# The second branch's merge gates as block products: eight projection slabs per half move into the row phase, and h transposed is written to DRAM

## The chip, the cores and the metric

The kernel runs on one core of one Trainium2 chip. TensorE (PE) multiplies, its weight loads are shown apart (PEld), VectorE (DVE) and ScalarE (ACT) do the elementwise work, GpSimd (POOL) helps both and issues its own DMAs, and SyncE (SP) issues most DMAs. Each engine takes its instructions in the order in which they stand in its queue. The metric is the device time of one launch in microseconds. Before the change the median of three runs is 2776.74 us (2776.49 to 2776.75). What a measurement of this kernel can tell from no change is about 0.2%.

## The reference

One layer of a streaming encoder, in float32, on 2048 prompt frames and 64 sample frames of width 1024:

```
h = rmsnorm(x, norm_g)
[q | k | v | g_a | u | g_b | m] = h @ w_in              # m: two gates of 1024 columns
att = stick_breaking(q, k, v)                           # 8 heads x 128
pb  = multi_scale_pool(u, state) @ w_pool * pool_scale  # windows 2, 4, 8, 16
y_a = (att * silu(g_a)) @ w_br_a
y_b = (pb  * silu(g_b)) @ w_br_b
gate = sigmoid(m)
x = x + (gate[:, :1024] * y_a + gate[:, 1024:] * y_b) @ w_out
y = rmsnorm(x, final_g)
```

The merge gates are the two halves of `sigmoid(m)`: columns 0 to 1023 gate the first branch, columns 1024 to 2047 the second. The sample frames attend to 4096 cached positions as well. Keys, values and the last 15 pooling inputs are outputs too.

## The kernel before, in words

**Numbers.** Every float32 product is made of three fp32r products: each operand is split by `split` (L81, L82) into a rounded part `hi` (ACT) and a rest `lo` (DVE or POOL), and PE adds hi*hi, lo*hi and hi*lo. A matmul here has a 128x128 stationary operand and up to 512 moving columns.

**Halves.** The 2112 rows of activations are worked on in two halves: half A has 1088 rows (1024 prompt rows and the 64 sample rows, in groups of 512, 256 and 320 columns), half B 1024 (two groups of 512). For each half h is built transposed in SBUF (`hhi`, `hlo`): x is loaded and normalised, four PE transposes turn a 128x512 block into the PSUM tile `tr` (two buffers), `split` takes it out (`transposed_h`, L207 on). `build_h0` does so for half A at the very start, `build_h1` for half B in the middle of the kernel.

**Projections.** `proj` (L278) makes 128 output columns of `h @ w_in` for a half, called a slab here: its weights are loaded (`raw`) and split (`whi`, `wlo`), then come 24 matmuls for every group of columns, into the PSUM tile `pj` (two buffers), and an evacuation. For the merge gates `gate_evac` takes a sigmoid on ACT into an `out` tile (L302; three buffers, shared by all that leaves through `outgoing`) and stores it to the DRAM tensor `sm_d`. There are sixteen such slabs per half, eight for each branch.

**What sets the order.** PE's order is written by hand, by generators that `run` interleaves in proportion to their nominal PE time. The order of the other engines is made by a scheduler in the front part of the program, and by hand in the back part. The front part is, in order: the build of h for half A with the first head's projections; attention of half A head by head, with the next head's projections between; the sample attention (`sample_stream`, 36 units of scores, transposes and products, nominal 104.2 us), interleaved with 28 slabs (six branch gates, four pooling groups of two slabs, fourteen merge gates); two more merge gates, interleaved with `build_h1`; attention of half B; branch gates and the pooling groups of half B; and fifteen merge gates (one stands before them), beside which `before_closing` prepares the first weights and rows of the back part.

**A sample unit.** PE makes scores of two heads (`z`, L737 and L738), ACT and DVE fold them into `be` (L742, L743), ACT takes two sigmoids (L569, L570), POOL copies the carry (L574, L581), DVE scans (L579) and multiplies (L582), PE transposes (L770), ACT and DVE split (`a`), and PE multiplies with the split values (L787). A pooling group adds on DVE, for each piece of its two slabs, log2(window) shifted sums (L333) with a few small ones beside them, a combination (L342), a split (`plo`), and later, after PE's mapping products (L388 to L390), a scaling (L392).

**The back part** begins with the row phase: for each branch and each of three strips of 704 rows, seven products of 512x512 blocks (an algorithm that replaces eight block products by seven with sums before and after). `order` lists (branch, strip, product); a step is one such product, 4 x 12 matmuls of 352 columns (`product`, L986 on). Rows come from DRAM (`aT_d`, `bT_d`) as blocks `r11` to `r22`, DVE makes their sums, `make` splits them two steps ahead. `emit` adds, multiplies with the gate loaded from `sm_d` (`sg`), for the second branch adds the first's result (`mp_d`), and stores by a DMA of POOL's queue. Weight blocks and four differences of them (`tw_d`, made by `weight_sums` on POOL or `sums_step` on DVE) are loaded and split by `forms`; `weights_at` says at which half step. After it come the output projection by the same seven products, and the last norm.

## Time and profile before

| what | value |
|---|---|
| median of three runs | 2776.74 us |
| the profiled execution | 2775.71 us, its span 2774.0 us |
| PE busy | 2706.2 us, 98% of the span |
| PEld busy | 2364.5 us |
| DVE busy | 1835.5 us, 66% |
| ACT busy | 1268.3 us, 46% |
| POOL busy | 582.6 us, 21% |
| HBM read, written | 232.46 MB, 108.65 MB |

Stages, by the times of their PE instructions in us from the start of the span: build of h for half A until about 57, attention of half A to 606, sample attention with its slabs to 1067, two merge gates and the build for half B to 1130, attention of half B to 1920, pooling of half B and the first merge gate to 2100, merge gates to 2259, row phase from 2259.87 to 2584.4, output after it.

In a row of the stage view the pairs are busy time and number of instructions of an engine in that stretch, followed by the granted PE clock (1.00 is full speed), the busy share of the DMA engines and what they moved. In a row of a group: source line, engine, operation, output<-inputs, shape and count, then busy time, mean duration in ns and idle time before, with what ended it. In a row of the timeline: start, duration, engine, line, operation, and in brackets the engine's idle time before it and what ended that.

### The profile page before, as it was taken

The numbers are of one execution on the slowest core, as the hardware profiler recorded it, in microseconds if no ns is written. First come the engines' busy times: TensorE is split into PE (matmuls) and PEld (weight loads), VectorE is DVE, ScalarE is ACT, GpSimd is POOL, SyncE is SP. The second block draws the span as 40 slices with busy tenths as digits, with TensorE's granted clock in tenths as the row PEclk, the third lists the DMA queues.
The fourth block names the chain that finished last, engine by engine and source line by source line (L and its number), as shares of the span: only waits on it lengthen the run. The fifth ranks groups of instructions, "written<-read, shape, count | busy, mean of one in ns | idle before, by whom it ended". The sixth has DMA issues, their size and how long they took to land.

```text
span 2774.0 us, 41821 instructions
## 1 busy us (share of the span) xinstructions
PE 2706.2 (98%) x15052; PEld 2364.5 (85%) x15052; DVE 1835.5 (66%) x2843; ACT 1268.3 (46%) x2520; POOL 582.6 (21%) x1285
## 2 busy tenths in 40 slices
PE   6999999999999999999999999999999999999898
PEld 6988888988998989888888888887778889999786
DVE  6555555567777684487878888886453237786776
ACT  4445444455555553355555555554222223333343
POOL 2112222220000001222432343331005501100001
PEclk9999999999999999999999999999999999999999
DMA  5224222234444544311111211112337848776653
GB/s 146 79 81 132 73 72 72 77 98 152 153 156 142 157 141 152 94 46 54 54 46 50 58 54 42 51 39 83 112 99 230 265 161 274 266 258 236 225 159 118
DMA packets 344397, 343.87 MB, mean 124 GB/s; under 512 B 30062, under 2 KB 286558, under 8 KB 344188
## 3 DMA queue, kind: packets, MB, share of 16 engines
q1 hardware_dynamic: 329756, 294.26, 34.2%
q0 software_dynamic: 14432, 46.93, 4.8%
q8 instruction: 118, 1.93, 0.3%
q14 instruction: 91, 0.75, 0.1%
HBM read 232.46 MB, written 108.65 MB: 123 GB/s over the span
## 4 chain that ended last, share of the span: by engine, by line
PE 84%; issue 6%; DVE 5%; DMA 2%; ACT 1%; POOL 1%; SPq 0%; POOLq 0%; DVEq 0%; ACTq 0%
PE pj L284 17%; PE pj L285 17%; PE pj L286 17%; PE tr L638 4%; PE att L655 2%; PE att L654 2%; PE z L627 2%; PE att L653 2%; PE z L626 2%; PE z L625 2%; PE x L989 2%; PE x L991 2%; PE x L993 2%; PE y L989 1%; PE y L993 1%
## 5 line engine op out<-in xcount | busy, mean ns | idle before, releaser
L284 PE MATMUL pj<-hhi,whi 128*128 128x512 f32 (+2 forms) x2608 | 946.5, 363 | 0.0
L286 PE MATMUL pj<-hhi,wlo 128*128 128x512 f32 (+2 forms) x2608 | 918.9, 352 | 0.5 <-DVE wlo L82 0.5
L285 PE MATMUL pj<-hlo,whi 128*128 128x512 f32 (+2 forms) x2608 | 917.7, 352 | 0.1
L286 PEld LDWEIGHTS pj<-hhi,wlo 128*128 128x128 f32 x2608 | 492.7, 189 | 66.1 <-DVE wlo L82 1.0
L284 PEld LDWEIGHTS pj<-hhi,whi 128*128 128x128 f32 x2608 | 495.5, 190 | 59.4 <-ACT hhi L81 0.2
L285 PEld LDWEIGHTS pj<-hlo,whi 128*128 128x128 f32 x2608 | 494.4, 190 | 59.3 <-DVE hlo L82 0.4
L579 DVE TENSOR_TENSOR_SCAN om<-om 128x513 f32<-128x513 f32 (+3 forms) x356 | 387.4, 1088 | 212.1 <-POOL om L561 108.3
L569 ACT ACTIVATE om<-z 128x512 f32<-128x512 f32 (+2 forms) x320 | 171.6, 536 | 322.3 <-PE z L627 272.7
L82 DVE TENSOR_TENSOR wlo<-raw,whi 128x512 fp32r<-128x512 f32 x248 | 179.7, 729 | 194.5 <-ACT whi L81 193.8
L581 POOL COPY carry<-om 128x1 f32<-128x1 f32 x356 | 78.6, 221 | 918.3 <-DVE om L579 870.7
L582 DVE TENSOR_TENSOR be<-be,om 128x512 f32<-128x512 f32 (+3 forms) x356 | 230.2, 647 | 31.5
L81 ACT CAST whi<-raw 128x512 fp32r<-128x512 f32 x256 | 158.2, 623 | 182.2 <-PE pj L285 164.3
L81 ACT CAST a<-tr 128x512 fp32r<-128x512 f32 (+2 forms) x356 | 188.0, 528 | 100.2 <-PE tr L638 89.6
L82 DVE TENSOR_TENSOR a<-tr,a 128x512 fp32r<-128x512 f32 (+2 forms) x356 | 215.2, 605 | 23.8 <-ACT a L81 21.6
L638 PE MATMUL tr<-ident,be 128*128 128x128 f32 x1088 | 175.6, 274 | 6.1 <-DVE be L582 3.6
L638 PEld LDWEIGHTS tr<-ident,be 128*128 128x128 f32 x1088 | 136.1, 140 | 44.7 <-DVE be L582 8.3
L570 ACT ACTIVATE be<-z 128x512 f32<-128x512 f32 (+2 forms) x320 | 170.0, 531 | 0.0
L653 PE MATMUL att<-a,v 128*128 128x512 f32 (+1 forms) x320 | 133.2, 416 | 0.0
L561 POOL TENSOR_SCALAR_AFFINE_SELECT om<-om 128x128 f32<-128x128 f32 x128 | 50.6, 395 | 354.0 <-ACT om L569 353.9
L574 POOL COPY om<-carry 128x1 f32<-128x1 f32 x224 | 124.0, 554 | 2.7 <-DVE be L582 0.7
L655 PE MATMUL att<-a,v 128*128 128x512 f32 (+1 forms) x320 | 118.4, 370 | 3.9 <-DVE a L82 3.6
L654 PE MATMUL att<-a,v 128*128 128x512 f32 (+1 forms) x320 | 117.3, 367 | 0.0
(312 smaller groups left out, 4681.1 us busy)
## 6 DMA issues: line engine op xcount, KB each, us to landing
raw<-in_w_in_dram SPq DMA_DIRECT2D x256, 256.0 KB, 3.2
sg<-sm_d SPq DMA_DIRECT2D x48, 352.0 KB, 5.7
kraw<-in_cache_k_dram SPq DMA_DIRECT2D x64, 256.0 KB, 3.6
vraw<-in_cache_v_dram SPq DMA_DIRECT2D x64, 256.0 KB, 2.9
sm_d<-sgm SPq DMA_DIRECT2D x48, 256.0 KB, 2.4
wraw<-tw_d SPq DMA_DIRECT2D x24, 512.0 KB, 4.1
out_dram<-nat SPq DMA_DIRECT2D x42, 256.0 KB, 2.3
r<-aT_d SPq DMA_DIRECT2D x12, 704.0 KB, 7.1
```

Source lines behind the costliest of these rows:

```text
L81: nc.scalar.copy(hi, src)
L82: (nc.gpsimd if eng == "g" else nc.vector).tensor_tensor(lo, src, hi.bitcast(F32), op=ALU.subtract)
L284: nc.tensor.matmul(ps[:, 0:n], whi[:, k], hhi[:, k, c0:c0 + n], start=k == 0, stop=False)
L285: nc.tensor.matmul(ps[:, 0:n], whi[:, k], hlo[:, k, c0:c0 + n], start=False, stop=False)
L286: nc.tensor.matmul(ps[:, 0:n], wlo[:, k], hhi[:, k, c0:c0 + n], start=False, stop=k == KT - 1)
L569: nc.scalar.activation(om[:, off:512], z[:, off:512], AF.Sigmoid, scale=-SCALE)
L579: nc.vector.tensor_tensor_scan(rev, rev, rev, 1.0, op0=ALU.mult, op1=ALU.bypass)
L582: nc.vector.tensor_tensor(be[:, off:512], be[:, off:512], om[:, off + 1:513], op=ALU.mult)
L638: nc.tensor.transpose(tr[:, i * P:(i + 1) * P], be[:, off + j * P:off + (j + 1) * P], ident)
L653: nc.tensor.matmul(self.acc[:, s], vhi[:, js], ahi[:, s], start=first, stop=False)
L654: nc.tensor.matmul(self.acc[:, s], vlo[:, js], ahi[:, s], start=False, stop=False)
L655: nc.tensor.matmul(self.acc[:, s], vhi[:, js], alo[:, s], start=False, stop=last)
```

## The change

The second branch's eight merge-gate slabs are taken out of both halves' projections. Its gates are computed in the back part instead, by the seven block products, as a new first pass of the row phase (21 steps, before the 42 of the two branches). For this the transposed h must be readable as rows from DRAM, so `transposed_h` gains an ACT copy of `tr` into an `out` tile (`ht`) and a store to the new tensor `hT_d`. The pass takes `hT_d` for its rows, the last 1024 columns of `w_in` for its weights; its `emit` takes a sigmoid on ACT instead of a product on DVE, and writes `sm_d` by POOL's queue. `weight_sums` of the new weights runs on POOL, listed beside the branch gates and pooling groups of half B. Those of the two branch weights, before on POOL beside the merge gates, move to DVE in the new pass (`own_at`, `own`: tiles of the tags `mp` and `mq`).

The list of slabs beside the sample attention is shortened from 28 to 20, with a weight of 22 in `run`; the last pooling group now ends that list.

```diff
-        def transposed_h(i, b, m, xt):
+        def transposed_h(half, i, b, m, xt):
...
             split(hhi[:, b * 4:b * 4 + 4, i * P:i * P + m], hlo[:, b * 4:b * 4 + 4, i * P:i * P + m],
                   trv[:, :, 0:m])
+            ht = outgoing("ht").rearrange("p (j r) -> p j r", j=4)
+            nc.scalar.copy(ht[:, :, 0:m], trv[:, :, 0:m])
+            c0 = half * RA + i * P
+            nc.sync.dma_start(hT_d[b * 512:(b + 1) * 512, c0:c0 + m].rearrange("(j p) r -> p j r", p=P), ht[:, :, 0:m])
...
-            rest.append(proj(GROUPS_A, [merge_gate(0, 3 * g)]))
+            rest += [proj(GROUPS_A, [merge_gate(0, c)]) for c in (2 * g,) if g < 3]
             rest.append(pool_group(0, g))
-            rest += [proj(GROUPS_A, [merge_gate(0, 3 * g + i)]) for i in (1, 2)]
-        rest += [proj(GROUPS_A, [merge_gate(0, c)]) for c in range(12, 2 * KT - 2)]
-        run((sample_stream(), SAMPLE_NS), (chain(*rest), 28.0 * pns))
-        fin = proj(GROUPS_A, [merge_gate(0, c) for c in (2 * KT - 2, 2 * KT - 1)])
+            rest += [proj(GROUPS_A, [merge_gate(0, c)]) for c in (2 * g + 1,) if g < 3]
+        run((sample_stream(), SAMPLE_NS), (chain(*rest), 22.0 * pns))
+        fin = proj(GROUPS_A, [merge_gate(0, c) for c in (KT - 2, KT - 1)])
...
-        run((chain(*rest), 1.0))
+        run((chain(*rest), 13.0), (weight_sums(0), 4.0))
...
-            yield from weight_sums(0)
-            yield from weight_sums(1)
...
-        run((chain(*[proj(GROUPS_B, [merge_gate(1, c)]) for c in range(1, 2 * KT)]), 15 * slab_ns(1)),
-            (before_closing(), 21.0))
+        run((chain(*[proj(GROUPS_B, [merge_gate(1, c)]) for c in range(1, KT)]), 7 * slab_ns(1)),
+            (before_closing(), 13.0))
...
-        order = [(i, t, p) for i in range(2) for t in range(3) for p in range(7)]
+        order = [(i, t, p) for i in range(3) for t in range(3) for p in range(7)]
...
-            src = (aT_d, bT_d)[i]
+            src = (hT_d, aT_d, bT_d)[i]
...
-            nc.vector.tensor_tensor(sg, src, sg, op=ALU.mult)
-            if i:
+            if i == 0:
+                sg = gates.tile([P, 2, NR], F32, name="sg", bufs=5)
+                nc.scalar.activation(sg, src, AF.Sigmoid)
+            else:
+                sg = sgs_.pop(n)
+                nc.vector.tensor_tensor(sg, src, sg, op=ALU.mult)
+            if i == 2:
                 nc.vector.tensor_tensor(sg, sg, mps.pop(n), op=ALU.add)
-            nc.gpsimd.dma_start((mp_d, m_d)[i][c * P:(c + 2) * P, rs].rearrange("(j p) r -> p j r", p=P), sg)
+            dst = (sm_d[D:2 * D], mp_d, m_d)[i]
+            nc.gpsimd.dma_start(dst[c * P:(c + 2) * P, rs].rearrange("(j p) r -> p j r", p=P), sg)
...
+        own_at = {4 * k + 4 * (i - 1) * 4: (i, k) for i in (1, 2) for k in range(4)}
```

**How instructions move, ACT in the first build of h.** The rows are ACT's after the squares of the first two row blocks; `hhi` is the cast out of `tr`, `jk` are sums of squares for later blocks, `sq` is the root that the next normalisation waits for. Before:

```order
L81 CAST hhi<-tr 128x4x128
L177 ACTIVATE jk,acc<-xt 128x512
L81 CAST hhi<-tr 128x4x128
L177 ACTIVATE jk,ss<-xt 128x512
L81 CAST hhi<-tr 128x4x128
L177 ACTIVATE jk,acc<-xt 128x512
L177 ACTIVATE jk,ss<-xt_260 128x512
L88 ACTIVATE sq_96<-sq_95 128x2
```

Now, with what each row waits for (line numbers in rows of the change are the changed file's, up to eight higher here):

```order
L82 CAST hhi<-tr 128x4x128 [waits PE_49]
L216 COPY ht<-tr 128x512 [waits DVE_49]
L178 ACTIVATE jk,acc<-xt 128x512 [waits DMAHW3_49]
L216 COPY ht<-tr 128x512 [waits DVE_49]
L82 CAST hhi<-tr 128x4x128 [waits PE_49]
L178 ACTIVATE jk,ss<-xt 128x512 [waits DMAHW4_49,Activation_49]
L82 CAST hhi<-tr 128x4x128 [waits PE_49]
L216 COPY ht<-tr 128x512 [waits DVE_49]
L178 ACTIVATE jk,acc<-xt 128x512 [waits DMAHW5_49,Activation_49]
L216 COPY ht<-tr 128x512 [waits DMAHW0_49,DVE_49]
L89 ACTIVATE sq_97<-sq_96 128x2 [waits DVE_49]
```

Four copies now stand ahead of the root, and each waits for DVE, which reads the same `tr` for `hlo` first.

**PE at the end of the sample attention.** `z` are a unit's scores, `tr<-ident,be` its transposes, `att` its products, `pj` are slabs. Before, the last unit's scores, transposes and products stand between slab matmuls:

```order
L770 MATMUL tr<-ident,be 128x128 x4
L284 MATMUL pj<-hhi,whi 128x512
L285 MATMUL pj<-hlo,whi 128x512
L286 MATMUL pj<-hhi,wlo 128x512
L284 MATMUL pj<-hhi,whi 128x512
L285 MATMUL pj<-hlo,whi 128x512
L286 MATMUL pj<-hhi,wlo 128x512
L787 MATMUL att<-v_12433,a_12563 128x256 x4
L787 MATMUL att<-v_12438,a_12563 128x256 x4
L284 MATMUL pj<-hhi,whi 128x256
```

Now the last unit runs with nothing between:

```order
L742 MATMUL z<-khi,q_10686 128x512
L743 MATMUL z<-klo,q2h 128x512
L407 MATMUL tr<-ident,shist 15x128
L775 MATMUL tr<-ident,be 128x128 x4
L792 MATMUL att<-v_11677,a_11944 128x256 x4
L792 MATMUL att<-v_11682,a_11944 128x256 x4
L775 MATMUL tr<-ident,be 128x128 x4
L792 MATMUL att<-v_11918,a_12036 128x256 x4
L792 MATMUL att<-v_11923,a_12036 128x256 x4
L792 MATMUL att<-v_12017,a_12052 128x256 x4
L792 MATMUL att<-v_12022,a_12052 128x256 x4
L289 MATMUL pj<-hhi,whi 128x512
```

The slabs ran out with the last pooling group, just ahead of these rows; only the two last merge gates follow.

**POOL in the last head of half B.** `om<-carry` and `carry<-om` are the copies that the scans wait for, `ws` and `tw_d` belong to `weight_sums(0)`. The rows are those of the last five units; before, this place held the copies alone:

```order
L895 DMA ws<-in_w_in_dram 128x512
L579 COPY om<-carry 128x1 x2
L586 COPY carry<-om 128x1
L897 TENSOR_TENSOR ws<-ws 128x512
L586 COPY carry<-om 128x1
L898 DMA tw_d<-ws 128x512
L897 TENSOR_TENSOR ws<-ws 128x512
L579 COPY om<-carry 128x1
L895 DMA ws<-in_w_in_dram 128x512
L898 DMA tw_d<-ws 128x512
L586 COPY carry<-om 128x1
```

Loads, subtractions and stores of the new weights now stand between the copies.

85 lines of the change are left out of this document (48 added, 37 removed).

## The prediction

> I forecast **no change that can be measured: 2776 us**, 0.7 us below the median before. TensorE gets 23 us less to do, and the order that goes with it gives about 22 us back as waits. "No change" means here within 0.2% (5.6 us), which is what a measurement of this kernel can tell.
>
> **What bounds the kernel now.** I read the page's sums and chain first, then the stages.
>
> ```profile
> PE 2706.2 (98%) x15052; PEld 2364.5 (85%) x15052; DVE 1835.5 (66%) x2843; ACT 1268.3 (46%) x2520; POOL 582.6 (21%) x1285
> PE 84%; issue 6%; DVE 5%; DMA 2%; ACT 1%; POOL 1%; SPq 0%; POOLq 0%; DVEq 0%; ACTq 0%
> ```
>
> ```profile
> 0.00:50.00 50.00, 28.30 (x170) 26.15 (x171) 35.69 (x76) 25.86 (x66) 17.68 (x38) 0.93 0.57 163
> 606.00:1067.00 461.00, 456.97 (x2899) 413.40 (x2898) 338.53 (x671) 249.07 (x500) 29.18 (x84) 1.00 0.49 154
> 1067.00:1130.00 63.00, 59.45 (x392) 55.62 (x392) 21.93 (x36) 19.70 (x40) 12.09 (x9) 0.95 0.39 118
> 2100.00:2260.00 160.00, 159.22 (x683) 127.79 (x682) 42.83 (x37) 40.59 (x66) 73.00 (x91) 1.00 0.67 216
> 2260.00:2422.00 162.00, 159.84 (x995) 159.28 (x996) 111.55 (x102) 52.62 (x51) 24.57 (x38) 1.00 0.79 268
> 2422.00:2585.00 163.00, 162.71 (x1024) 162.43 (x1023) 126.85 (x117) 58.01 (x57) 17.18 (x24) 1.00 0.76 258
> ```
>
> PE is the bound everywhere but in the first 50 us (28 of 50 busy). So a matmul removed is time gained, if whatever stood beside it still fits. It fits closely in one place: the sample stage, 606 to 1067, has DVE at 338.5 of 461 us, 73%.
>
> **PE's work.** In 2100:2260, which is all merge gates, 683 matmuls of 512 columns take 160 us: 234 ns each, 0.458 ns a column. Sixteen slabs go, eight of 24 x 1088 columns and eight of 24 x 1024: 405,504 columns, 185.6 us. The row phase is 995 + 1024 matmuls of 352 columns in 325 us, 161 ns each. The new pass is 21 steps x 48 = 1008 of them: 162.3 us. **Difference -23.3 us.** Its bounds are narrow (1% of either stage, 2 us).
>
> The Trainium skill speaks a little against the change here: "TensorE: Matmul & The Clock Gate", section "Wait — 56ns, not 53.3ns?", gives columns / 2.4 GHz + 2.5 ns, a fixed part that weighs more on 352 columns than on 512. By it the estimate would be 171.4 - 150.4 = -21.0 us. The rows run 8% above that rule for both widths, and no run here separates the fixed part.
>
> **First build of h.** Every `tr` tile is now read a third time, and the order shows the copy waiting for DVE's `hlo`.
>
> ```profile
> PE tr L211 <- DVE xt L204: 15.4, 2, 14.6
> PE tr L459 <- DVE hlo L82: 5.4, 2, 4.9
> ```
>
> ```profile
> 28.88 0.75 DVE L204 SCALAR_TENSOR_TENSOR xt<-xt,rstd,g_bc 128x512 f32<-128x512 f32 x1
> 29.55 0.48 DVE L201 TENSOR_SCALAR xt<-xt,rstd 128x512 f32<-128x512 f32 x1
> 30.60 1.49 DVE L201 TENSOR_SCALAR xt<-xt,rstd 128x512 f32<-128x512 f32 x1
> 47.89 0.69 DVE L82 TENSOR_TENSOR hlo<-tr,hhi 128x512 fp32r<-128x512 f32 x1 [1.43 <-ACT hhi L81]
> ```
>
> ```profile
> 20.22 0.64 ACT L177 ACTIVATE jk<-xt 128x512 f32<-128x512 f32 x1
> 21.46 0.20 ACT L88 ACTIVATE sq<-sq 128x2 f32<-128x2 f32 x1
> 47.27 0.59 ACT L81 CAST hhi<-tr 128x512 fp32r<-128x512 f32 x1
> ```
>
> A copy is priced as the cast of the same shape out of `tr`, 0.59 us. Four stand ahead of the root (21.46): 2.4 us less a small gap of ACT, 2.2. The wait of 4.9 us at L459 is for a `tr` buffer, released now by a copy after `hlo`: 0.6 more. From 42 to 57 us a buffer is held 0.6 + 0.59 + 0.69 + 0.59 us, and at five places two transposes stand close together: about 0.5 each, 2.5. The `out` ring (below) 0.7. **+6 us**; bounds 0 (all copies beside the waits that stand there already) and 17 x 0.59 = 10.
>
> **Sample stage.** Eight of 28 slabs go from beside 36 units (and two of them stand behind, as before). DVE loses only their `wlo` splits:
>
> ```profile
> L743 DVE TENSOR_TENSOR be<-z,be 64x512 f32<-64x512 f32 (+1 forms) x68 | 44.0, 647 | 21.5 <-ACT be L742 18.8 <-DMA kraw<-in_cache_k_dram 1.3
> L579 DVE TENSOR_TENSOR_SCAN om<-om 128x513 f32<-128x513 f32 (+1 forms) x34 | 38.8, 1142 | 15.0 <-ACT om L569 14.6
> L82 DVE TENSOR_TENSOR wlo<-raw,whi 128x512 fp32r<-128x512 f32 x52 | 35.5, 685 | 7.2 <-ACT whi L81 6.8
> ```
>
> 16 x 0.685 = 11 us of 338 go, while the stage shrinks by 8 x 11.95 us (24 x 1088 columns at 0.458) to 365: DVE at 90%. That is an average; the pooling groups lie above it, and where they do, PE already waits a little:
>
> ```profile
> 886.00:906.00 20.00, 18.82 (x117) 16.59 (x117) 18.91 (x54) 11.20 (x28) 1.06 (x4) 1.00 0.56 181
> 1006.00:1026.00 20.00, 19.05 (x120) 17.24 (x119) 19.11 (x54) 11.39 (x27) 0.37 (x2) 1.00 0.52 161
> ```
>
> Before, merge gates follow each group and DVE catches up. Now nothing follows the last group. From its first evacuation to the last unit's split DVE has 46 instructions of about 512 columns, 4 scans, 26 of about 256 and 30 small ones in its order. Their spacing when DVE is never idle:
>
> ```profile
> 1023.31 0.69 DVE L82 TENSOR_TENSOR klo<-tr,khi 128x512 fp32r<-128x512 f32 x1
> 1023.91 0.22 DVE L342 SCALAR_TENSOR_TENSOR s<-s,es 128x64 f32<-128x64 f32 x1
> 1024.04 0.43 DVE L333 TENSOR_TENSOR s<-s 128x264 f32<-128x264 f32 x1
> 1024.38 0.69 DVE L82 TENSOR_TENSOR klo<-tr,khi 128x512 fp32r<-128x512 f32 x1
> ...
> 1049.57 1.41 DVE L743 TENSOR_TENSOR be<-z,be 64x512 f32<-64x512 f32 x2 [1.75 <-ACT be L742]
> 1051.80 1.23 DVE L579 TENSOR_TENSOR_SCAN om<-om 128x513 f32<-128x513 f32 x1 [0.83 <-ACT om L569]
> 1053.13 0.69 DVE L582 TENSOR_TENSOR be<-be,om 128x512 f32<-128x512 f32 x1
> ```
>
> 0.60, 0.13 and 0.34 us, and 1.14 a scan: 27.6 + 4.6 + 8.8 + 3.9 = 45 us. With 0.6 to begin, 0.8 of waiting for the last sigmoids and the last 16 products (1.9): 48 us. PE has in the same stretch 52 matmuls of 512 columns, 108 of 256 and 48 of 320 (69,632 columns, 31.9 us) and ten groups of four transposes (4.4): 36 us. So PE waits 12 us, in the mapping products, then at `be` and `a` of the last two units. The third group, window 8, has by the same sum 41 us and 1.5 of waits against 39.6 of PE: 3 us. Some 2 us of the waits that stand there now go into these. **+13 us**; bounds 4 (the last unit's chain alone: 4.3 us from L743 to the end of L582 and 1.4 for `a`, less 1.5 of PE work between) and 20 (3.4 us more if the clock is withdrawn in the waits, as in the next row, and the same again in the second group).
>
> **Second build of h.** Sixteen copies again, and their stores stand in SP's order between the loads of x.
>
> ```profile
> 1106.00:1130.00 24.00, 20.52 (x150) 20.20 (x149) 12.62 (x22) 8.48 (x19) 10.18 (x8) 0.86 0.35 109
> ```
>
> ```profile
> PE tr L211 <- DVE hlo L82: 3.5, 1, 3.5
> ```
>
> ACT has room (8.5 of 24 us); three close pairs of transposes cost 0.5 each. The load of V's weights now stands earlier against the x loads, which may end the 3.5 us wait. **+1.5 us**, bounds -3.5 and 16 x 0.59 = 9.
>
> **Last head of half B.** POOL gets loads (0.54 us to issue) and subtractions (1.3) between the carry copies:
>
> ```profile
> 2111.53 0.54 POOL L904 DMA_DIRECT2D ws<-in_w_br_a_dram  x1 [2.98 <-DMA tw_d<-ws]
> 2113.76 1.29 POOL L906 TENSOR_TENSOR ws<-ws 128x512 f32<-128x512 f32 x1 [1.69 <-DMA ws<-in_w_br_a_dram]
> ```
>
> ```profile
> 1901.68 0.67 POOL L574 COPY om<-carry 128x1 f32<-128x1 f32 x1
> 1904.10 0.19 POOL L581 COPY carry<-om 128x1 f32<-128x1 f32 x1 [1.75 <-DVE om L579]
> 1904.21 0.66 POOL L574 COPY om<-carry 128x1 f32<-128x1 f32 x1
> 1909.91 0.19 POOL L581 COPY carry<-om 128x1 f32<-128x1 f32 x1 [3.03 <-DVE om L579]
> ```
>
> The last copy (1904.2) is needed by a scan that begins near 1908.7 (1.2 us before its carry copy), so 4 us of cover; I count one landing (2.2), two subtractions and three issues in front of it, 6.4 us, of which 1.9 us in POOL's gaps: **+0.5 us**, bounds 0 and 13 (five subtractions, 12 issues, none covered).
>
> **Back part.** The closing of the front has seven slabs (78 us) for twelve loads and splits, each 4.1 us and 1.2 through two buffers: 32 to 40 us, covered. In the new pass DVE loses 24 products of 0.8 us and gains 16 subtractions of 0.6 over what the first pass has now (111.5 of 162 us); ACT gains 24 sigmoids (52.6 of 162). Behind a late `own` load on DVE stand row splits that PE needs two steps (15 us) on. **+1.5 us**, bounds -1.2 (the gate loads that go from its start) and 8.
>
> **Sum.** -23.3 + 6 + 13 + 1.5 + 0.5 + 1.5 = -0.8 us, against the span of 2774.0, whose execution is 2775.71 and lies 1.0 below the median: 2776 us.
>
> **The rivals.**
> (1) The waits are hidden, faster. DVE at 95% costs PE only 1 us in 20 in the two rows above, and PE's two tiles let it run ahead. Then the sample stage costs its lower bound, 4, the first build 3 and the rest 2: 2776.7 - 23.3 + 9 = 2762. Against it: in those rows light slabs follow. Chance with all of its kind (below 2771): 0.32.
> (2) The `out` ring binds in both builds, slower. Three tiles serve `ht`, `nat` and gates:
>
> ```profile
> sm_d<-sgm SPq DMA_DIRECT2D x48, 256.0 KB, 2.4
> out_dram<-nat SPq DMA_DIRECT2D x42, 256.0 KB, 2.3
> ```
>
> At 0.6 + 0.4 + 2.3 us a tile and three tiles, one leaves each 1.1 us; 28 in the first build's 40 us and 30 in the second's 45 need 1.4 and 1.5. It decides once a store needs more than 3.2 us from issue to landing. At 5 us (SP held by other waits) it is 2.0 us a tile: 56 and 60 us, +16 and +15 in place of 7.5, so 2800. Chance 0.14.
> (3) POOL's new rows hold the scans of the last head: 2776 + 12 = 2788. The 1.49 against 0.48 us of L201 above falls together with POOL's product on the same blocks; if DVE's multiply after each scan meets POOL's subtractions likewise, 1.3 us more each time. The Trainium skill, "SBUF — State Buffer", "SBUF: two separate sides", has such pairs exclude each other for whole instructions; the L201 row agrees. Chance 0.05.
> (4) The change doesn't do what it says: the new pass runs slower than 161 ns, because loads for `own` (8 x 1 MB on a DMA share of 0.79) delay rows: +8 and more, 2785. Chance 0.07.
>
> **How the numbers follow.** Forecast (2771 to 2782) 0.42. Faster 0.32 is rival 1. Slower 0.26 is rivals 2 to 4. Between the bounds the sum could go from -24 to +37, but not all terms go one way; the root of the summed squares of their half widths is 14, so 8 in 10 reach from 2762, which takes in rival 1, to 2790, which takes in 3 and 4. The forecast's own range is 2771 to 2782.
>
> **What would show it.** PE pj matmuls fall by 8 x 72 + 8 x 48 = 960 and 1008 of 352 columns come, 161 ns apart. The sample stage, first scores to last products, shrinks by 80 us or so and not by 93; its waits stand at L393 and at the last transposes and products, on DVE's `plo`, `be` and `a`. The first head's scores begin 6 us later. It is wrong if these waits are below 5 us in sum, if L211's successor waits for DMAs of `out` tiles, or if the row phase is over 490 us long.

## The result

The changed kernel takes 2792.23 us (median, 2791.68 to 2797.86) against 2776.61 us of the kernel before in the same series: ratio 1.0063, 95% interval 1.0051 to 1.0075. It is **slower by 15.6 us**. The forecast was 2776 with a range to 2790, so the time lies outside the range.

The page of the changed kernel, its sums and the chain that ended last:

```profile
PE 2695.0 (97%) x15100; PEld 2372.2 (85%) x15100; DVE 1912.0 (69%) x2908; ACT 1315.2 (47%) x2559; POOL 580.1 (21%) x1293
PE 78%; DVE 8%; issue 7%; ACT 2%; DMA 2%; POOL 1%; SPq 0%; POOLq 0%; DVEq 0%; ACTq 0%
```

PE is 11 us less busy, and its share of the chain falls from 84% to 78% while DVE's rises from 5% to 8%. PE's work went down as forecast; its waits went up by more.

**By stage.** The next table is worked out from PE's records in the two profiled executions. A stage runs from its first matmul to that of the next. "Work" is each matmul's distance to the next one's start at the median of its kind in the kernel before, summed; "lost" is the rest: waits, and stretches at a lower clock.

```
stage                        length before  after   change    work    lost
build of half A                  89.42      93.53    +4.1      0      +4.1
attention A                     516.66     516.31    -0.4      0      -0.4
sample stage                    461.14     401.97   -59.2    -78.9   +19.8
second build                     98.88      84.34   -14.5    -16.6    +2.0
attention B                     754.42     758.72    +4.3      0      +4.3
pooling B and merge gates       339.36     251.87   -87.5    -88.8    +1.3
row phase                       324.84     497.32  +172.5   +161.3   +11.2
out phase to the span's end     189.29     186.83    -2.5      0      -2.5
sum                            2774.0     2790.9    +16.9    -23.0   +39.8
```

The work is what was forecast (-23.0 for -23.3), counted at the prices of the kernel before. The losses are 40 us for a forecast of 22.5. Half of them are in the sample stage, a quarter in the row phase. (The 2.5 us gained at the end lie behind the last product; what they are was not looked into.)

Not all that is lost is waiting. In short windows the granted clock is either 1.00 or 0.50, and it is 0.50 for 3.4 us or for two or three times that. Half of PE's busy time in such stretches is 2.5 us of the sample stage's loss, 1.7 of attention B's and 3.9 of the row phase's. In the kernel before, up to the end of the row phase, only the two builds have such stretches (3.0 and 2.8 us; 2.6 and 1.5 now).

**The sample stage.** Windows of the changed kernel: length, busy time of PE, PEld, DVE, ACT and POOL, granted clock, DMA share, GB/s. The first row is the whole stage, the second its end, the third most of the second build, the fourth the start of the row phase.

```profile
610.00:1012.00 402.00, 382.88 (x2421) 343.34 (x2419) 324.51 (x657) 229.52 (x467) 27.89 (x83) 0.99 0.50 157
...
980.00:1012.00 32.00, 22.66 (x134) 20.02 (x133) 28.55 (x70) 14.93 (x34) 4.05 (x6) 0.89 0.56 173
1012.00:1061.00 49.00, 43.07 (x302) 40.06 (x301) 21.29 (x36) 23.66 (x48) 13.13 (x10) 0.97 0.71 213
...
2106.00:2160.00 54.00, 50.06 (x296) 48.60 (x296) 30.26 (x28) 20.93 (x23) 8.51 (x14) 0.97 0.82 277
```

DVE's share of the stage rises from 73% to 81%. In its last 32 us DVE is busy for 28.6 and PE idle for 9.3, at a mean clock of 0.89. PE's waits in the stage (in all, times, longest):

```profile
PE z L393 <- ACT phi L82: 3.6, 3, 1.8
PE tr L775 <- DVE be L587: 3.5, 1, 3.5
PE tr L407 <- DVE shist L373: 2.7, 2, 2.1
PE tr L407 <- DVE s L338: 2.3, 3, 1.1
PE att L792 <- DVE a L83: 2.3, 1, 2.3
```

These are the waits that the forecast named for the last units and the pooling groups. The last 32 us lose 13.1 of the stage's 29.8 us, the rest of the stage 16.7; in the kernel before all of its 9.9 us are lost ahead of the last 32. The order also has 45 of the units' instructions on PE in a row near the end, without a projection matmul between them: the list beside the units holds 20 slabs and is paced as 22, so it ends when the units are 20/22, 91%, done.

**The last head of half B.** Compared instruction by instruction, attention B runs within 0.2 us of the kernel before for 724 us and loses 4.1 us in the last 30. POOL, then DVE, then PE there:

```profile
1839.99 1.28 POOL L897 TENSOR_TENSOR ws<-ws 128x512 f32<-128x512 f32 x1 [2.37 <-DMA ws<-in_w_in_dram]
1841.22 0.18 POOL L579 COPY om<-carry 128x1 f32<-128x1 f32 x1
```

```profile
1841.43 1.23 DVE L584 TENSOR_TENSOR_SCAN om<-om 128x513 f32<-128x513 f32 x1 [1.56 <-POOL om L579]
```

```profile
1843.51 0.33 PE L643 MATMUL tr<-ident,be 128*128 128x128 f32 x1 [1.93 <-DVE be L587]
```

```profile
1840.00:1856.00 16.00, 14.07 (x63) 10.72 (x62) 5.79 (x8) 4.01 (x7) 11.20 (x16) 0.89 0.68 228
```

POOL waits 2.4 us for a landing, subtracts for 1.3, and only then makes the copy that the last scan needs. PE waits 1.9 us. The mean clock of 0.89 in the last row is 3.4 us at 0.50, from 1843.8 on, which cost 1.7 more. With some shorter waits these are the 4.1.

**The start of the row phase.** DVE at its first seven steps, and PE's waits in the whole phase:

```profile
2157.59 0.68 DVE L932 TENSOR_TENSOR ws<-ws 128x512 f32<-128x512 f32 x1
2160.28 2.14 DVE L932 TENSOR_TENSOR ws<-ws 128x512 f32<-128x512 f32 x3 [2.00 <-DMA ws<-in_w_br_a_dram]
2162.34 1.22 DVE L956 TENSOR_TENSOR t4lo<-wraw,t4hi 128x1024 fp32r<-128x1024 f32 x1
```

```profile
PE x L1001 <- DVE t4lo L956: 3.5, 1, 3.5
PE y L999 <- DVE rlo L83: 1.2, 1, 1.2
PE x L999 <- DVE rlo L83: 1.1, 1, 1.1
```

DVE's subtractions for `own` (L932) wait for a load and stand ahead of the split of t4, which PE needs at 2158. The steps take 9.4, 10.8, 7.8 and 14.4 us there (the third, fourth, sixth and seventh) where 7.6 is the rule; the third took 9.3 in the kernel before too. The clock is 0.50 for 3.4 us from 2133.9 and for 6.8 us from 2161.2, behind the waits in the fourth and the seventh step.

**The builds.** PE's waits up to 62 us:

```profile
PE tr L464 <- ACT ht L216: 6.9, 4, 5.8
PE tr L212 <- ACT ht L216: 2.6, 2, 1.4
```

Where the kernel before waited 5.4 us for `hlo` it now waits 6.9 for the copy behind it, and twice more for a copy at L212.

### The profile page after: what moved, and what is told of

Same layout as the page of the kernel before. It is cut to its first block, busy times and chain, and to the rows that moved or that the text cites. A ratio compares the mean times of both kernels' runs of the same rounds, so it can differ in the third digit from the quotient of the medians.

```text
span 2790.9 us, 42169 instructions
## 1 busy us (share of the span) xinstructions
PE 2695.0 (97%) x15100; PEld 2372.2 (85%) x15100; DVE 1912.0 (69%) x2908; ACT 1315.2 (47%) x2559; POOL 580.1 (21%) x1293
## 3 DMA queue, kind: packets, MB, share of 16 engines
q8 instruction: 119, 1.95, 0.3%
## 4 chain that ended last, share of the span: by engine, by line
PE 78%; DVE 8%; issue 7%; ACT 2%; DMA 2%; POOL 1%; SPq 0%; POOLq 0%; DVEq 0%; ACTq 0%
PE pj L289 14%; PE pj L290 14%; PE pj L291 13%; PE tr L643 4%; PE x L997 3%; PE x L1001 3%; PE x L999 3%; PE att L660 2%; PE att L659 2%; PE att L658 2%; PE y L1001 2%; PE y L997 2%; PE z L632 2%; PE y L999 2%; PE z L631 2%
## 5 line engine op out<-in xcount | busy, mean ns | idle before, releaser
L289 PE MATMUL pj<-hhi,whi 128*128 128x512 f32 (+2 forms) x2288 | 831.3, 363 | 0.0
L291 PE MATMUL pj<-hhi,wlo 128*128 128x512 f32 (+2 forms) x2288 | 805.9, 352 | 0.5 <-DVE wlo L83 0.5
L290 PE MATMUL pj<-hlo,whi 128*128 128x512 f32 (+2 forms) x2288 | 804.6, 352 | 0.1
L291 PEld LDWEIGHTS pj<-hhi,wlo 128*128 128x128 f32 x2288 | 432.8, 189 | 57.6 <-DVE wlo L83 1.0
L289 PEld LDWEIGHTS pj<-hhi,whi 128*128 128x128 f32 x2288 | 435.3, 190 | 50.8
L290 PEld LDWEIGHTS pj<-hlo,whi 128*128 128x128 f32 x2288 | 434.3, 190 | 51.0 <-DVE hlo L83 0.4
L83 DVE TENSOR_TENSOR wlo<-raw,whi 128x512 fp32r<-128x512 f32 x216 | 150.4, 701 | 123.7 <-ACT whi L82 123.0
L83 DVE TENSOR_TENSOR a<-tr,a 128x512 fp32r<-128x512 f32 (+2 forms) x356 | 215.1, 605 | 25.2 <-ACT a L82 23.3
L83 DVE TENSOR_TENSOR rlo<-r,rhi 128x1408 fp32r<-128x1408 f32 x52 | 84.3, 1622 | 79.9 <-ACT rhi L82 79.9
L658 PE MATMUL att<-a,v 128*128 128x512 f32 (+1 forms) x320 | 133.4, 417 | 0.0
L82 ACT CAST rhi<-r 128x1408 fp32r<-128x1408 f32 x52 | 71.3, 1371 | 113.3 <-PE y L1001 50.7
```

The source lines that it names most:

```text
L82: nc.scalar.copy(hi, src)
L83: (nc.gpsimd if eng == "g" else nc.vector).tensor_tensor(lo, src, hi.bitcast(F32), op=ALU.subtract)
L289: nc.tensor.matmul(ps[:, 0:n], whi[:, k], hhi[:, k, c0:c0 + n], start=k == 0, stop=False)
L290: nc.tensor.matmul(ps[:, 0:n], whi[:, k], hlo[:, k, c0:c0 + n], start=False, stop=False)
L291: nc.tensor.matmul(ps[:, 0:n], wlo[:, k], hhi[:, k, c0:c0 + n], start=False, stop=k == KT - 1)
L658: nc.tensor.matmul(self.acc[:, s], vhi[:, js], ahi[:, s], start=first, stop=False)
```

## The experiments

Times are medians, ratios are to the kernel before in the same series. The diffs are against the changed kernel unless said otherwise. A difference of less than 0.2% (5.6 us) between two of these kernels is more than their times can tell; there the profiles have to show it. Steps of the row phase that are given by number are counted from 0.

### The copies of h alone

The kernel before with L215 to L218 of the change and the DRAM tensor.

> The kernel before, with the copies and stores of h transposed alone (33 copies on ACT out of the transposes' tiles, 33 stores to a DRAM tensor that nobody reads). Theory: they cost what the two builds lost in the changed kernel, 4.1 us up to the first scores and 1 to 2 in the second build, so the time rises by 5 to 6 us to 2781. Rival: part of the loss in the builds came from the other lists and the queues of the changed kernel; then it is below 3 us.

2785.2 us, ratio 1.0032 (1.0020 to 1.0044). The profiled execution (span 2781.7, 7.7 longer) has the first scores at 93.35 in place of 89.42 (+3.9), the second build 2.4 longer, and 1.6 more in attention B, all in its first 60 us. Waits of its first build:

```profile
PE tr L464 <- ACT ht L216: 7.1, 4, 5.9
PE tr L212 <- ACT ht L216: 2.6, 2, 1.4
```

The builds' losses are the copies'. The 1.6 us of attention B are not: they are 3.4 us at half clock behind a wait of 1.94 us that the kernel before has too, without such a stretch. By the times the copies cost 9 us, more than the 5 to 6 expected; the profile shows where 6 of them are.

### h stored by POOL, later

```diff
-            nc.scalar.copy(ht[:, :, 0:m], trv[:, :, 0:m])
+                    parts = [x[:, b * 4:b * 4 + 4, i * P:i * P + m].bitcast(F32) for x in (hhi, hlo)]
+                    nc.gpsimd.tensor_tensor(ht[:, :, 0:m], *parts, op=ALU.add)
...
-                    (stats1(), 8.0) if half == 0 and hd == 2 else (None, 0))
+                    (stats1(), 8.0) if half == 0 and hd == 2 else (keep_h(half), 18.0 - 2 * half) if hd == 4 else (None, 0))
```

`keep_h` is the loop over the blocks of a half around these lines, the `ht` tile and its store. The gate weights' sums are moved as in the next experiment.

> The changed kernel with the gate weights' sums beside the merge gates (2788.6 us by itself), and h transposed no longer copied by ACT in the two builds: POOL adds the two parts of h out of SBUF in the fifth head of each half, 18 and 16 additions of 1.3 us and their stores. Theory: the builds lose their 4.1 and 2 to 3 us because a transposes' tile is held for a third reader; with it gone they are what they were (first scores at 89.4, second build's waits 7.6), attention stays as it is, and the time falls by 6 to 2782 to 2783. Rival: POOL's additions hold carry copies, or exclude DVE, in that head, as the gate weights' sums did in the last one; then attention loses 4 us or more in each half and nothing is gained.

2785.6 us, ratio 1.0033 (1.0021 to 1.0044); 3.0 below the run with the sums alone moved. The first build is as before the change:

```profile
PE tr L471 <- DVE hlo L83: 6.2, 2, 4.4
PE tr L212 <- ACT nat L473: 0.7, 1, 0.7
```

First scores at 89.8, the second build 5.2 us shorter than in the run with the sums alone moved. Both readings were right in part: attention A loses 0.9 us, attention B 5.8, at PE's waits for `be` and `a` in the fifth head. So half A's copies are better made by POOL, half B's are not.

### The gate weights' sums out of the last head

```diff
-        run((chain(*rest), 13.0), (weight_sums(0), 4.0))
+        run((chain(*rest), 1.0))
...
-            (before_closing(), 13.0))
+            (before_closing(), 13.0), (weight_sums(0), 12.0))
```

> The changed kernel, with the gate weights' sums (POOL) taken out of the last head and the pooling stage and put beside the seven merge gate slabs, in the tiles that the kernel before used for them there. Theory: POOL's loads and subtractions hold the carry copies of the last head's scans (attention of half B 758.7 us against 754.4 before, all of it lost in its last 15 us) and delay the pooling stage by another 2 us. Then attention B is 754.5 again, the 2.0 us of waits for `hist` are gone, and the time falls by 4 to 6 us to about 2787. Rival: the sums now come too late for t1 and t2; SP's queue holds at their loads, and the row phase begins 5 us or more later: no gain, 2790 or more.

2788.6 us, ratio 1.0047 (1.0030 to 1.0064): 3.6 us better, less than the times can tell. The last 30 us of attention B are those of the kernel before to within 0.1 us:

```profile
1840.00:1856.00 16.00, 15.99 (x77) 12.32 (x77) 7.68 (x12) 6.43 (x12) 1.65 (x3) 1.00 0.40 132
```

The pooling stage gains too: its length to the row phase is 249.9 us, and 249.8 to 250.1 in the three other kernels with this edit, against 251.1 to 256.3 in the ten with the sums where the change put them. In those POOL subtracts beside DVE's pooling sums, and PE waits up to 3 us for `hist` at L407. The rival is half right as well, in SP's queue (start, length, engine, line):

```profile
2069.70 14.54 SPq L949 DMA_DIRECT2D wraw<-tw_d  x2
...
2093.51 10.45 SPq L311 DMA_DIRECT2D sm_d<-sgm  x3
2105.68 2.67 SPq L1090 DMA_DIRECT2D r<-hT_d  x4
```

It begins the rows' loads 2 us after the row phase's first matmul, but so did the changed kernel (2108.8 and 2106.7).

### The list beside the samples: its pace

```diff
-        run((sample_stream(), SAMPLE_NS), (chain(*rest), 22.0 * pns))
+        run((sample_stream(), SAMPLE_NS), (chain(*rest), 20.0 * pns))
```

> The changed kernel, with the list beside the sample attention paced by 20 slabs (what it holds) in place of 22, so that it no longer ends before the units do. Theory A: the sample stage loses 20 us because the last units stand alone on PE (45 instructions in a row with no projection matmul between) while DVE is behind; with the list stretched to the end these waits shrink by half, 2792 falls to about 2782. Theory B: the pooling group's DVE work is what has to be done at the end, wherever the units stand; then the waits only move from the last units to the mapping products and the build of half B behind them, and the time stays within 3 us of 2792.

2785.5 us, ratio 1.0037 (1.0022 to 1.0052): 6.7 us better, more than theory B allows and less than A expected. Sample stage and second build together lose 32.0 us (17.6 in the kernel before, 39.4 in the changed one), the last 32 us of the sample stage 1.8 in place of 13.1. Without the stretches at half clock the two stages lose 25.7, 14.8 and 35.4: the pace is worth 10 us of waits.

### The list's order

The pace of 20, and

```diff
-            rest += [... merge_gate(0, c) ... for c in (2 * g,) if g < 3]
             rest.append(pool_group(0, g))
-            rest += [... merge_gate(0, c) ... for c in (2 * g + 1,) if g < 3]
+            rest += [... merge_gate(0, c) ... for c in (2 * g - 2, 2 * g - 1) if g > 0]
```

> As the run paced by 20 slabs, and the six merge gate slabs stand in pairs behind the second, third and fourth pooling group, so that no pooling group ends the list. Theory B (a pooling group with no light slab behind it leaves DVE a backlog that PE waits for): the sample stage's 20 us of waits and slow clock fall to 4 or 5, the time to about 2777. Theory A alone (units standing alone): no better than the run paced by 20 slabs. Theory C (DVE at 90% of the stage is the bound wherever the groups stand): 2 to 4 us better than the changed kernel, no more.

2789.2 us, ratio 1.0050 (1.0035 to 1.0065). The loss is 33.0 us, no less than with the pace alone (31.3 and 25.7 without the stretches at half clock). What stands behind the last pooling group is not what the stage loses by. The waits are spread over all of it, 15 of 0.3 to 2.5 us, at `kraw`, `s`, `gbl`, `a` and `as`.

### DVE relieved, by POOL and by ACT

Two kernels with the pace of 20. In the first POOL makes the low parts of the sample values and of the light slabs' weights; in the second ACT writes the whole values in the place of their low parts, so that DVE's subtraction is left out:

```diff
-                        split(v[:, :, :, 0, :], v[:, :, :, 1, :], rv)
+                        split(v[:, :, :, 0, :], v[:, :, :, 1, :], rv, "g")
```

(and "g" for the twelve light slabs' `proj`), and

```diff
-                        split(v[:, :, :, 0, :], v[:, :, :, 1, :], rv)
+                        nc.scalar.copy(v[:, :, :, 0, :], rv)
+                        nc.scalar.copy(v[:, :, :, 1, :], rv)
```

> As the run paced by 20 slabs, and beside the sample attention POOL makes the low parts of the sample values (two of 128 x 512 a unit) and of the light slabs' weights, which take about 60 us off DVE in the stage. Theory C: DVE, busy over 80% of the stage, is what the small waits all over it come from; the stage with the second build, 478.9 us paced by 20 slabs against 464.4 without waits, falls by 6 to 10 us, the time to 2778. Rival: a POOL subtraction and a DVE one of two operands on SBUF exclude each other, so that DVE is as late as before; then no more than 2 us are gained, and DVE's `be` and `plo` take longer for one.

> As the run paced by 20 slabs, and ACT writes the low parts of the sample values as plain copies (the output is then not the reference's), so that DVE has two subtractions of 0.64 us a unit less, 41 us over the stage, and POOL gets nothing. Theory C: the waits that pacing left (sample stage and second build: 32 us beyond the matmuls' own pace, against 17.6 in the kernel before) come from DVE's share; they fall to 22 to 26 and the time from 2785.5 to 2777 to 2780. Rival: they come from loads and from ACT's part of the chain; then ACT's extra 1.2 us a unit makes it no better, 2785 or more.

POOL: 2801.2 us, ratio 1.0097 (1.0080 to 1.0114). ACT: 2781.8, ratio 1.0019 (1.0010 to 1.0028). The sample stage of the run with the pace alone, with POOL, and with ACT:

```profile
611.00:987.00 376.00, 364.56 (x2307) 327.69 (x2305) 305.67 (x598) 225.62 (x450) 25.00 (x81) 0.99 0.51 160
```

```profile
610.00:1001.00 391.00, 369.41 (x2311) 330.74 (x2310) 295.29 (x518) 225.76 (x451) 138.02 (x164) 0.98 0.50 154
```

```profile
611.00:980.00 369.00, 360.29 (x2309) 324.90 (x2308) 272.24 (x538) 255.13 (x511) 25.16 (x81) 1.00 0.53 163
```

With ACT, DVE's share falls from 81% to 74% and the loss of sample stage and second build from 32.0 to 24.0. That is in the range of theory C; the time lies between it and the rival. Of the 8.0 us, 4.6 are stretches at half clock that stand in the run with the pace alone and not in this one, and two later kernels with the same pace and all of DVE's work lose 27.6 and 30.3. So **33 us less of DVE's work are worth 4 to 8 us, some 3 of them waits.** That DVE's share sets the loss is not shown: with POOL it is 76%, and the loss is the largest of all. There DVE does 80 instructions less and is busy only 10 us less, since the others take longer. DVE's groups with the pace alone (busy, mean ns), then with POOL:

```profile
L587 DVE TENSOR_TENSOR be<-be,om 128x512 f32<-128x512 f32 (+1 forms) x36 | 22.9, 635 | 2.0 <-ACT be L575 0.3
L338 DVE TENSOR_TENSOR s<-s 128x256 f32<-128x256 f32 (+7 forms) x30 | 14.6, 486 | 0.2
```

```profile
L587 DVE TENSOR_TENSOR be<-be,om 128x512 f32<-128x512 f32 (+1 forms) x35 | 25.8, 737 | 2.1
L338 DVE TENSOR_TENSOR s<-s 128x256 f32<-128x256 f32 (+7 forms) x26 | 16.7, 642 | 0.3
L83 POOL TENSOR_TENSOR v<-vraw,v 128x512 fp32r<-128x512 f32 x59 | 82.8, 1420 | 28.9 <-ACT v L82 28.6
```

The operations take 16% and 32% longer (the second with a slightly different mix of shapes), and the stage loses 45.6 us with the second build. The 64 splits klo<-tr,khi, which read a PSUM tile, keep their time (687 and 686 ns). The Trainium skill, "SBUF — State Buffer", section "SBUF: two separate sides", has a GpSimd instruction and a VectorE instruction with two SBUF inputs exclude each other for whole instructions; the run agrees, and it ends the idea of giving POOL such work beside a busy DVE.

### The row phase without `own`, and `own` elsewhere

Five kernels, each an edit of `own_at` or of the loads. Without `own`:

```diff
-        own_at = {4 * k + 4 * (i - 1) * 4: (i, k) for i in (1, 2) for k in range(4)}
+        own_at = {}
...
-                src = tw_d[i, int(nm[1]) - 1]
+                src = tw_d[3 if i == 3 else 0, int(nm[1]) - 1]
```

> The changed kernel without the `own` steps: no sums of the two branches' weights in the row phase, the products of both branches take the gates' sums in their place (the output is then not the reference's); loads and splits of weights and rows are as before. Theory: the row phase's waits (13.4 us beyond the pace of its matmuls, 2.2 in the kernel before) come from `own`, through SP's queue or DVE's; without it they are 3 to 5, the row phase is 488 and the time 2783. Rival: the twelve loads and splits ahead of the pass and the rest of the weights' forms are late by themselves; the stalls at steps 2 to 6 stay and the row phase is above 494.

Left out: the row phase is 488.8 us and loses 4.9 us where the changed kernel loses 13.4 and the kernel before 2.2. PE's waits in it:

```profile
PE x L999 <- DVE rlo L83: 1.2, 1, 1.2
PE x L997 <- DVE sg L1149: 1.1, 2, 0.9
PE x L997 <- issue: 0.8, 1, 0.8
PE x L1001 <- DVE t4lo L956: 0.7, 1, 0.7
```

So `own` costs 8.5 us of the phase: 3.9 of them are the stretches at half clock, of which this run has none in the phase. The six other kernels with `own` at the same places lose 12.8 to 16.6 us. The seventh step still takes 9.6 us; that the loads and splits ahead of the pass, with only seven slabs for cover, are the cause is not shown. No run has the loads of `own` without its subtractions, so their shares are not separated. (The time, 2786.3, ratio 1.0036, 1.0023 to 1.0048, is 5.9 below the changed kernel's. The profiled execution, the slowest of six, is only 1.1 us shorter: it lost 7.4 us elsewhere, 4.0 of them in the pooling stage.)

```diff
+        own_at = {12 + 4 * k + 4 * (i - 1) * 4: (i, k) for i in (1, 2) for k in range(4)}
```

> The changed kernel, with all eight `own` steps twelve half-steps later in the row phase (first at 12 in place of 0); nothing else moves. Theory: the row phase of the changed kernel (first product to the out phase 497.3 us, against 63 steps of 7.63 = 480.7) loses about 10 us in its steps 2, 3, 5 and 6 because DVE's `own` subtractions, and the loads they wait for, stand ahead of the splits of rows and of t3, b22 and t4. Then the row phase falls to 488 or so, the wait on t4lo (3.5 us) is gone, and the time falls from 2792 to about 2784. Rival: seven slabs are too little cover for the splits ahead of the pass and the weights come late whatever DVE does; then the same steps lose the same 10 us and the time stays at 2792.

Twelve half-steps later: 2792.8 us, ratio 1.0065 (1.0050 to 1.0080), no gain. The stalls at the start shrink to those of the run without `own`, and others come at the change to the next pass, steps 20 to 23. DVE there, then PE:

```profile
2289.09 2.86 DVE L932 TENSOR_TENSOR ws<-ws 128x512 f32<-128x512 f32 x4
2291.88 1.22 DVE L956 TENSOR_TENSOR t3lo<-wraw,t3hi 128x1024 fp32r<-128x1024 f32 x1
2293.01 1.62 DVE L83 TENSOR_TENSOR rlo<-r,rhi 128x1408 fp32r<-128x1408 f32 x1
```

```profile
2294.68 0.61 PE L999 MATMUL x<-rlo,t2hi 128*128 128x352 f32 x1 [3.65 <-DVE rlo L83]
```

Just before these rows DVE had waited 5.1 us for a load of rows (`aT_d`), which has its part in this stall.

```diff
+        own_at = {h: (i, k) for i, at in ((1, (10, 15, 20, 25)), (2, (30, 36, 42, 48))) for k, h in enumerate(at)}
```

> The changed kernel, with the `own` steps at half-steps 10, 15, 20, 25 and 30, 36, 42, 48 of the row phase in place of every fourth from 0. Theory: what holds the start of the row phase is SP's queue. An `own` load waits there until POOL's stores of the step before have landed (84 us of waits in SP's queue between 2100 and 2320 of the changed kernel, 61 with the steps moved by twelve but still four apart, where the stalls only moved to steps 20 to 23), and the loads of rows and weights stand behind it. Four half-steps are 15.3 us, and load, wait, subtraction and store need about 15. At five or six apart SP no longer waits, the row phase falls from 497.3 to 488 and the time from 2792 to 2783. Rival: it is DVE's subtractions themselves, wherever they stand; then the stalls move with them again and the row phase stays above 495.

Spaced: 2800.2 us, ratio 1.0086 (1.0071 to 1.0101). SP's waits at `own` loads between 2100 and 2320 fall from 84.2 us to 36.6 and the row phase loses 16.3 us, most of it in steps 23 and 24 (10.9). Fewer waits in SP's queue did not help.

```diff
-                        nc.sync.dma_start(b, weights[i][r:r + P, j * 512:(j + 1) * 512])
+                        nc.gpsimd.dma_start(b, weights[i][r:r + P, j * 512:(j + 1) * 512])
```

> The changed kernel, with the loads of `own` issued by POOL's queue in place of SP's; their places and DVE's subtractions are unchanged. Theory that SP's queue is what stalls the pass (loads of rows and weights stand behind `own` loads that wait for stores): the row phase's waits fall from 13.4 to 5 to 8 us and the time to 2784 to 2787. Rival, DVE's order: its subtractions wait for loads that come no earlier, ahead of splits; then the row phase stays at 495 or more, and the time at 2790 or more.

POOL's queue: 2795.8 us, ratio 1.0071 (1.0056 to 1.0086); the row phase loses 13.1 us. SP's waits at `own` loads are gone and the phase loses as much, so they are not what it loses by, as my theory had it. But the stalls are not the same: the rows land later, and the second step takes 10.6 us. In the changed kernel and in the runs that moved `own`, what the profiles show at most of the stalls is `own` on DVE in front of a split or a sum for which PE, or ACT and then PE, waits.

```diff
+        own_at = {h: (i, k) for i, at in ((1, (12, 16, 20, 24)), (2, (51, 55, 59, 63))) for k, h in enumerate(at)}
-        sums_at = {53 + 4 * k: (3, k) for k in range(4)}
+        sums_at = {96 + 4 * k: (3, k) for k in range(4)}
```

> The changed kernel, with the `own` steps at half-steps 12, 16, 20, 24 (first branch) and 51, 55, 59, 63 (second), and the output weights' sums at 96 to 108: no clump stands among the forms of a pass's weights (0 to 10, 28 to 50, 70 to 94). Theory: a clump costs only there, since PE then waits for a sigmoid or a split that stands behind it; the row phase falls to 488 to 490, with the stalls at steps 2 and 6 alone left, and the time to 2783 to 2785. Rival: a clump costs wherever it stands; the stalls turn up near steps 25 to 32 or 48 to 55, and the row phase stays at 495 or more.

Between the forms: 2793.0 us, ratio 1.0055 (1.0042 to 1.0069). In the profiled execution (span 2787.8, 3.1 shorter) the two first passes have the stalls of the run without `own` and no others; with the output weights' sums moved as well, 3.0 us are lost at steps 56 and 59. The row phase loses 8.3 us in place of 13.4, but 3.9 of the difference are the stretches at half clock, which did not come in this execution. The time shows no gain, so that placing `own` between the forms pays stays open.

### All together

The pace of 20, the gate weights' sums beside the merge gates, `keep_h` for half A alone, and

```diff
+        own_at = {h: (i, k) for i, at in ((1, (11, 15, 19, 23)), (2, (27, 31, 35, 50))) for k, h in enumerate(at)}
```

> The changed kernel with four edits together: the list beside the sample attention paced by 20 slabs (6.7 us by itself), the gate weights' sums beside the merge gates (3.6), half A's h transposed stored by POOL in the fifth head in place of ACT's copies in the first build (3.7 less in the build, 1 more in attention in the run that did both halves), and the `own` steps at half-steps 11, 15, 19, 23, 27, 31, 35 and 50, which keeps them off the start of the pass (steps 0 to 5) and off the change to the next pass (steps 20 to 24), the two places at which they cost something in the runs that moved them. Theory: a clump of `own` costs only where the splits of rows and weights stand close together; then the row phase is 489 to 491 (488.8 without `own`), and the sum is 2792.2 - 6.7 - 3.6 - 2.7 - 7 = 2772, which would be level with the kernel before or just below it (2776). Rival: `own` costs wherever it stands; then the row phase stays at 496 or more and the time at 2779.

2774.1 us, ratio 0.9998 (0.9989 to 1.0007): level with the kernel before. First scores at 89.9, sample stage and second build lose 27.6 us, attention B is 754.35 and pooling 250.1. The row phase has not changed: it loses 14.1 us, with one wait of 3.5 at step 20 for a sigmoid on ACT, at the end of a chain of DVE and ACT that begins behind an `own` clump.

> The combined kernel with the same places for `own` and the output weights' sums. Theory: 2774.1 less 7 to 9 us, 2766, faster than both kernels (before 2775.5) by 0.3%. Rival: no better than 2773.

2769.6 us, ratio **0.9973** (0.9962 to 0.9983): faster than the kernel before by 0.27% and than the changed one by 22.6 us. The row phase still loses 12.3 us, 5.5 of them at its second and third step. SP's queue there, DVE's first sum of rows, and the same sum in the changed kernel:

```profile
2091.53 3.84 SPq L1102 DMA_DIRECT2D r<-hT_d  x4
```

```profile
2100.79 1.62 DVE L1107 TENSOR_TENSOR s<-r,r 128x1408 f32<-128x1408 f32 x1 [14.71 <-DMA r<-hT_d]
```

```profile
2115.43 1.63 DVE L1095 TENSOR_TENSOR s<-r,r 128x1408 f32<-128x1408 f32 x1 [12.19 <-ACT x L1012]
```

The rows' loads begin 2 us after the row phase did (2089.6), as in the changed kernel (2106.7). But DVE can begin its sum only 11.2 us after that start, 8.7 there: the loads land later. Why they do is open.

## Why the prediction was wrong

**PE's work: right.** -23.0 us for -23.3: the matmuls that went and came are those counted. Both figures use prices of the kernel before; where the rows ran slower than that, it is in the losses.

**First build: right in kind, a little less.** +4.1 for +6, within 0 to 10; 3.9 with the copies alone, gone with POOL making them.

**Second build: the number right, in part by luck.** +2.0 for +1.5; 2.4 with the copies alone. Without the stretches at half clock it loses 8.1 us where the kernel before lost 4.9, so the copies cost 3 us of waits; the kernel before had 6.8 us at half clock there and the changed one 3.4.

**Sample stage: mis-sized, +19.8 for +13, at the end of its bounds (20).** The tail's price came out: 12 us were forecast for the last group and the last units, and the last 32 us lose 13.1, 2.5 of them by the clock, at the places named. But the group's place was not the reason: paced by 20, with the same group last, the last 32 us lose 1.8. I saw in the order that the last group came last, and did not read off the 22 against 20 slabs that nothing at all would stand beside the last 9% of the units. The step that failed is the rest of the stage: 3 us for the third group less 2 of old waits, where it loses 6.8 more than before, in waits all over it. DVE's work is part of that, since 33 us less of it are worth 4 to 8; what makes up the remainder is open. Of the 19.8, 7 to 8 are the pace. The order of the groups, on which the term rested, gained nothing.

**Last head: the mechanism right, mis-sized, +4.3 for +0.5.** The step was "4 us of cover" for 6.4 us in front of the last copy, less 1.9 in POOL's gaps. PE's wait was 1.9 us; that half clock for 3.4 us would follow it, and that the same subtractions would slow the pooling stage behind it by 1 to 4 us, was not in the term. Rival 3 gave 12 us to this place with a chance of 0.05; it was 4.3.

**Back part: wrong, +12.5 for +1.5, beyond its bound of 8.** The failed sentence is "Behind a late `own` load on DVE stand row splits that PE needs two steps (15 us) on". What stands behind it are also the splits of t3, b22 and t4, which the order puts into the same first ten half-steps, and these PE needs at once. 8.5 of the row phase's 11.2 are `own`, 3.9 of them by the clock, for which the term had nothing. The price of a clump stood in the kernel before: its four sums for the output weights cost PE 0.9 us at step 13 (see the last section). The sign that the forecast named for itself, a row phase over 490 us, came: 497.3. Rival 4 ("loads for `own` delay rows: +8 and more", 2785, chance 0.07) had the right place; the waits are for DVE's order more than for the DMA share that it named, as far as the profiles show.

**Rival 1** (waits hidden, 2762) was wrong in the sample stage above all: two rows in which DVE at 95% cost PE 1 us in 20 were taken as a rule for the stage. **Rival 2** (the `out` ring) did not come: what PE waits for in the builds is the copy, not a store. (In the second build the profile names nothing that ended five of these waits, 5.4 us; the two longest end 0.1 us after a copy.)

**The range.** Four terms of five that could only lose came out above their values, and three of them in the same way, as DVE or POOL work came to stand in front of what PE needs next. Only the sample stage's bound had a term for the clock; the changed kernel has 6 us more of it up to the end of the row phase. I added the half widths as if they were independent. Only the sum of the upper bounds (37 us) held them.

## What to carry to other kernels

Work taken off the bound engine gives back its time only where the engine next in line has room: look up that engine's share in the stage that shrinks, after the change and not before. It is a warning and not a price: at the same 81% the stage here lost 21.7 or 29.9 us, by the pace of the list. Small clumps of work in an in-order queue cost by what stands right behind them, so list what the next engine needs within the following ten microseconds before a place is called free. When a list that fills another's gaps gets shorter, its pace has to be shortened with it. And a wait of the bound engine is to be priced with the stretch at a lower clock that may follow it.

## What the runs showed of the hardware

**Half clock, in slices of 3.4 us.** In each of the sixteen profiled executions all stretches at half clock begin on one grid with a step of 3.413 us. Take the time from 70 us to the end of the row phase in slices of that grid, and of these the ones at full clock. PE was idle for 1.95 us or more in 51 of them, and half clock followed every one. It was idle for 1.45 to 1.93 us in 53, and half clock followed 12. It never followed a slice with less. So what a wait costs depends on where it falls: the wait of 1.94 us at the start of attention B stands in all sixteen, and costs 1.7 us more in the seven in which it lies in one slice. It is split in the changed kernel (first two rows) and whole in the run with the gate weights' sums moved (last two):

```profile
1103.07:1106.48 3.41, 1.66 (x8) 1.40 (x9) 3.20 (x4) 0.88 (x2) 1.30 (x4) 1.00 0.02 5
1106.48:1109.89 3.41, 3.41 (x18) 2.82 (x17) 2.58 (x4) 1.68 (x4) 0.84 (x3) 1.00 0.00 0
```

```profile
1103.33:1106.74 3.41, 1.35 (x8) 0.79 (x7) 3.07 (x4) 1.19 (x3) 1.77 (x5) 1.00 0.00 0
1106.74:1110.15 3.41, 3.41 (x10) 2.54 (x9) 1.90 (x3) 0.48 (x1) 0.78 (x2) 0.50 0.02 5
```

The Trainium skill, "TensorE: Matmul & The Clock Gate", "Part 1: The HAM clock gate (the "warmup" mystery)", lets the clock fall after an idle window of about 3.4 us; here 1.95 us of idle time in a slice of that length were enough.

**Several paces of the same matmuls.** A step of 48 matmuls of 352 columns takes 7.63 us (158.9 ns each), 7.68 (160.0) or 7.73 (161.1) at a granted clock of 1.00, and keeps its pace over tens of steps; in the row phases looked at it changes only at a stall. In the changed kernel 27 steps at 7.73 make 2.7 us; with `own` between the forms 20 steps run at 7.68. What sets the pace is open.

**A clump that was there before.** One step of the row phase takes 8.81 us in the kernel before (step 13) and in the changed one (step 34). DVE, then PE, in the changed kernel:

```profile
2385.95 2.86 DVE L932 TENSOR_TENSOR wraw<-wraw 128x512 f32<-128x512 f32 x4
2388.72 1.68 DVE L1149 TENSOR_TENSOR sg<-x,sg 128x704 f32<-128x704 f32 x2
```

```profile
2389.75 0.40 PE L997 MATMUL x<-rhi,b11hi 128*128 128x352 f32 x1 [0.93 <-DVE sg L1149]
```

Four sums for the output weights stand on DVE ahead of the product with the gate, which reads the tile `x` that PE needs next. PE waits 0.9 us, as it did at the same clump in the kernel before.
